# A decoder block on one core: the feed-forward by seven block products for eight

## The chip, the cores and the metric

The kernel runs on one core of a Trainium2 chip. The metric is the device time of one execution in microseconds (us). TensorE multiplies matrices out of on-chip memory into PSUM, VectorE and ScalarE do the elementwise work, GpSimd does a little of it, and SyncE issues most transfers between DRAM and on-chip memory. In the rows of a profile they are called PE, DVE, ACT, POOL and SP. PEld is the load of a matmul's stationary operand, which overlaps PE.

## The reference

One layer of a decoder over 512 tokens of width 2048: two token mixers side by side, an output projection, and a gated feed-forward of inner width 5632. The change touches the last part, from `w_out` on.

```python
def reference(x, norm_mix_g, w_in, sink_logits, w_branch_a, w_branch_b, w_out,
              norm_ffn_g, w_ffn_in, w_ffn_down, norm_final_g):
    ...
    x = x + (sigmoid(ga) * ya + sigmoid(gb) * yb) @ w_out
    h = rmsnorm(x, norm_ffn_g)
    gate, up = jnp.split(h @ w_ffn_in, 2, axis=-1)
    x = x + (silu(gate) * up) @ w_ffn_down
    return rmsnorm(x, norm_final_g)
```

All of it is float32. `x` is 512 x 2048, `w_ffn_in` 2048 x 11264, `w_ffn_down` 5632 x 2048.

## The kernel before

**Every product is three matmuls.** Each float32 operand is kept as a high part, rounded to the type fp32r, and the low part that is left over. A product is hi·hi + hi·lo + lo·hi. A weight block of 128 x 1024 elements (512 KB) is brought by one SP transfer (L130), cast to its high part by ACT (L134), and the low part is formed by DVE (L135). Three buffers each hold the raw block, its high and its low part (`wp`). `Weights.next` keeps two blocks ahead of the one in use. One such block feeds 24 matmuls of 512 columns in the feed-forward.

**Feed-forward.** The normalised `x2`, features on partitions, stands as sixteen pairs `fh`, `fl` of 128 x 512. The inner width is walked in five parts, `FF_PARTS` = 8, 8, 8, 10, 10 tiles of 128. In a part, `features` (L208 to L210) computes two tiles of gate and then two of up, with the weights stationary and the features moving. `scaled` (L353) multiplies by the reciprocal norm of each token, which `along_rows` had spread over all partitions as `inv2_bc`; ACT takes silu (L818), DVE multiplies (L824), ACT and DVE split the result into `ah` and `al` (L826, L827). Then `rows` (L722 to L724) multiplies `ah`, `al` (stationary) by the rows of `w_ffn_down` (moving), four token tiles for each of four column blocks, and DVE adds the four banks to `x2` (L843). The last column block of the last part is written out by hand: the weights are split ahead (`split_tail`), and token tile after token tile is finished, normalised and sent out (L858 to L864, `finish`).

**What sets the order.** The weights are planned as a list in the order of use. The program is recorded in code order and then put in an order by a scheduler, after which each engine runs its own rows strictly in that order; a row that waits holds up every row behind it on its engine. `later` and `gap` put small pieces of work between weight blocks.

**Before the feed-forward.** `w_out` is multiplied by `rows` for four column blocks n. After each block `x2` is added up (L753), squared (L730), transposed 128 x 128 by 128 x 128 (`turn_x1`; by DVE and copies for the first twelve feature tiles, by PE for the last four) and split into `fh`, `fl` (L254, L255).

On-chip memory: 79 slots of 128 x 512 in one pool (`tp`), constants in `cp`. PSUM has eight banks, four tagged "mm" and four "at".

Of the kernel before, what the change touches and what calls it, by code (L numbers as in the profile page):

```python
# [16 lines left out]
P = 128  # L17
T = 512
# [23 lines left out]
FF_PARTS = (8, 8, 8, 10, 10)  # L42
# [3 lines left out]
def kernel(  # L46
# [22 lines left out]
    tp = ctx.enter_context(tc.tile_pool(name="tp", bufs=79))  # L69
# [42 lines left out]
    class Weights:  # L112
# [11 lines left out]
        def split(self):  # L124
            w, k0, nk, c0, ncol = self.todo.popleft()
            raw = wp.tile([P, 1024], F32, tag="raw", name=uid("raw"))
            hi = wp.tile([P, 1024], F32R, tag="whi", name=uid("whi"))
            lo = wp.tile([P, 1024], F32R, tag="wlo", name=uid("wlo"))
            n = nk * ncol
            nc.sync.dma_start(  # L130
                out=raw[:, :n].rearrange("p (k c) -> p k c", k=nk),
                in_=w[k0 * P : (k0 + nk) * P, c0 : c0 + ncol].rearrange("(k p) c -> p k c", p=P),
            )
            nc.scalar.copy(hi[:, :n], raw[:, :n])  # L134
            nc.vector.tensor_tensor(out=lo[:, :n], in0=raw[:, :n], in1=f(hi[:, :n]), op=ALU.subtract)  # L135
            self.ready.append(
                (
                    hi[:, :n].rearrange("p (k c) -> p k c", k=nk),
                    lo[:, :n].rearrange("p (k c) -> p k c", k=nk),
                    nk,  # L140
                )
            )

        def next(self):
            while self.todo and len(self.ready) <= self.AHEAD:
                self.split()
            return self.ready.popleft()
# [28 lines left out]
    f0 = 0  # L176
    for p, nf in enumerate(FF_PARTS):
        for g in range(nf // 2):
            plan_cols(w_fi, KD, (f0 + 2 * g) * P)
            plan_cols(w_fi, KD, DFF + (f0 + 2 * g) * P)  # L180
        for n in range(4 if p < len(FF_PARTS) - 1 else 3):
            plan_rows(w_fd, f0, nf, n)
        f0 += nf
# [67 lines left out]
    def split_features(b, g):  # L251

        hi, lo = slot("fh", F32R), slot("fl", F32R)
        upper.append(nc.scalar.activation(out=hi, in_=b, func=AF.Copy, scale=g))  # L254
        nc.vector.scalar_tensor_tensor(out=lo, in0=b, scalar=g, in1=f(hi), op0=ALU.mult, op1=ALU.subtract)  # L255
        return hi, lo
# [70 lines left out]
    for b, base in enumerate((0, P)):  # L327
        df = const(f"dist{b}", 2 * P)
# [16 lines left out]
    inv_bc, invq_bc = const("inv_bc", T), const("invq_bc", T)  # L345
# [238 lines left out]
    corner = [[const(f"corner{e}{j}", 2 * P, F32R) for j in range(2)] for e in range(2)]  # L584
# [103 lines left out]
    for g in range(8):  # L688
# [11 lines left out]
        for m in range(2):  # L700
# [3 lines left out]
            mh[k], ml[k] = slot("mh", F32R), slot("ml", F32R)  # L704
# [27 lines left out]
    def turn_x1(k, tag):  # L732
        if k < KD - 4:
            z = slot("z")
            for t in range(NT):
                nc.vector.transpose(
                    z[:, t * P : (t + 1) * P], x2[t][k // 4][:, (k % 4) * P : (k % 4 + 1) * P]
                )
            fh[k], fl[k] = split_features(unblock(z, NT, 8), gcol[:, KD + k : KD + k + 1])
            return  # L740
        b = bank(tag)
        for t in range(NT):
            transpose(b[:, t * P : (t + 1) * P], x2[t][k // 4][:, (k % 4) * P : (k % 4 + 1) * P])
        fh[k], fl[k] = split_features(b, gcol[:, KD + k : KD + k + 1])

    for n in range(4):
        tag = ("mm", "at")[n % 2]
        for t in range(NT):
            x2[t][n] = load_after("x2", x[t * P : (t + 1) * P, n * T : (n + 1) * T], v)
        ob = [bank(tag) for _ in range(NT)]  # L750
        rows(KD, mh, ml, ob)
        for t in range(NT):
            nc.vector.tensor_tensor(out=x2[t][n], in0=x2[t][n], in1=ob[t], op=ALU.add)  # L753
            square_of(x2[t][n], ss2[:, 4 * t + n : 4 * t + n + 1])
        v = x2[0][n]
        for k in range(4 * n, 4 * n + 4):
            later(lambda k=k, tag=tag: turn_x1(k, tag), 4 if n < 3 else 2)

    def norm2():
        inv2 = const("inv2", NT)  # L760
        nc.vector.tensor_reduce(out=inv2, in_=ss2.rearrange("p (t c) -> p t c", t=NT), axis=AX.X, op=ALU.add)
        rsqrt_mean(inv2, inv2, NT, [small(s, NT) for s in ("rv", "rr", "rq")])
        nc.scalar.copy(inv2_bc, along_rows(inv2))

    inv2_bc = cp.tile([P, T], F32, tag="inv_bc", name="inv2_bc")


    later(norm2, 2)
    sst = const("sst", 4 * NT + 1)
    tail_w = []  # L770
    gf = [None] * 4

    def split_tail(k):

        raw = wp.tile([P, 1024], F32, tag="raw", name=uid("raw"))
        nc.sync.dma_start(
            out=raw.rearrange("p (k c) -> p k c", k=2),
            in_=w_fd[k * P : (k + 2) * P, 3 * T :].rearrange("(k p) c -> p k c", p=P),
        )
        for j in range(2):  # L780
            r = raw[:, j * T : (j + 1) * T]
            a, b = slot("dh", F32R), slot("dl", F32R)
            nc.scalar.copy(a, r)
            nc.vector.tensor_tensor(out=b, in0=r, in1=f(a), op=ALU.subtract)
            tail_w.append((a, b))

    def tail_next():
        if len(tail_w) < FF_PARTS[-1]:
            split_tail(KF - FF_PARTS[-1] + len(tail_w))

    def finish(t):

        tot, inv = small("tot", 1), small("inv3", 1)
        nc.vector.tensor_reduce(
            out=tot, in_=sst[:, 4 * t : 4 * t + (5 if t == NT - 1 else 4)], axis=AX.X, op=ALU.add
        )
# [8 lines left out]
    f0 = 0  # L805
    for p, nf in enumerate(FF_PARTS):
        last_part = p == len(FF_PARTS) - 1
        ah, al = [], []
        for g in range(nf // 2):
            gbk = [bank("mm") for _ in range(2)]  # L810
            features(KD, fh, fl, gbk)
            if p == 0 and g == 0:
                while pieces:
                    pieces.popleft()[1]()
            sl = []
            for m in range(2):
                v = scaled(gbk[m], inv2_bc)
                nc.scalar.activation(out=v, in_=v, func=AF.Silu)  # L818
                sl.append(v)
            ub = [bank("mm") for _ in range(2)]  # L820
            features(KD, fh, fl, ub)
            for m in range(2):
                u = scaled(ub[m], inv2_bc)
                nc.vector.tensor_tensor(out=u, in0=u, in1=sl[m], op=ALU.mult)  # L824
                a, b = slot("ah", F32R), slot("al", F32R)
                nc.scalar.copy(a, u)  # L826
                nc.vector.tensor_tensor(out=b, in0=u, in1=f(a), op=ALU.subtract)  # L827
                ah.append(a)
                al.append(b)
        if last_part:  # L830
            for n in range(4):
                gf[n] = load_after("gf", norm_final_g[n * T : (n + 1) * T].partition_broadcast(P), f(al[-1]))
        for n in range(4):
            tag = ("at", "mm")[n % 2]
            banks = [bank(tag) for _ in range(NT)]
            if last_part and n == 3:
                break
            if last_part and n >= 1:
                for k in range(nf // 2):
                    later(tail_next, 2)  # L840
            rows(nf, ah, al, banks)
            for t in range(NT):
                nc.vector.tensor_tensor(out=x2[t][n], in0=x2[t][n], in1=banks[t], op=ALU.add)  # L843
                if last_part:
                    square_of(x2[t][n], sst[:, 4 * t + n : 4 * t + n + 1])
                    nc.vector.tensor_tensor(out=x2[t][n], in0=x2[t][n], in1=gf[n], op=ALU.mult)
        if last_part:
            extra = bank("at")
            for t in range(NT):
                c = slice(t * P, (t + 1) * P)  # L850
                if t < NT - 1:
                    parts = [(banks[t], slice(0, T))]
                else:
                    parts = [(banks[t][:, : T // 2], slice(0, T // 2)), (extra[:, : T // 2], slice(T // 2, T))]
                for e, (b, cols) in enumerate(parts):
                    for k in range(nf):
                        wa, wb = tail_w[k]
                        mm(b, lhsT=ah[k][:, c], rhs=wa[:, cols], start=(k == 0), stop=False)  # L858
                        mm(b, lhsT=ah[k][:, c], rhs=wb[:, cols], start=False, stop=False)  # L859
                        mm(b, lhsT=al[k][:, c], rhs=wa[:, cols], start=False, stop=(k == nf - 1))  # L860
                    xt = x2[t][3][:, cols]
# [41 lines left out]
```

## Time and profile before

| | |
|---|---|
| time, median of 3 runs | 2655.57 us (2654.2 to 2655.95) |
| the profiled execution | 2655.02 us |
| its span in the trace | 2653.1 us, 1.9 us less than its time |
| feed-forward in the trace | from about 1185 us to about 2642 us |
| full-width matmuls of the feed-forward | 4224 in gate/up, 2112 in down |
| `w_ffn_in` loads | 176 of 512 KB |
| `w_ffn_down` loads | 88 of 512 KB |
| DMA traffic over the span | 284.18 MB, mean 107 GB/s |

The span is the time from the first to the last thing that the trace holds of this execution. Busy times are sums over an engine's instructions; several matmuls are in flight at once, so the mean duration of one (389 ns for 512 columns) is longer than the distance from one to the next. The distance is read from a stretch in which PE never pauses. "Idle before" is the time an engine stood still ahead of the rows of a group, and the name behind the arrow is what ended most of it.

### The profile page before, as it was taken

How to read it: one execution, taken by the hardware profiler on the slowest of the kernel's cores; microseconds unless marked ns; L12 is line 12 of the kernel's file. 1: busy time of each engine (PE TensorE's matmuls, PEld its weight loads, DVE VectorE, ACT ScalarE, POOL GpSimd, SP SyncE). 2: the span in 40 equal slices, each digit the busy share in tenths (PEclk: the TensorE clock that was granted, in tenths of full speed). 3: DMA queues.
4: the chain of work that ended last, by engine and by line, in shares of the span. 5: the costliest groups of instructions: out<-in, count | busy, mean ns of one | idle time of the engine just before them, and what ended most of it. 6: DMA issues, size and time to landing. Idle time of an engine off the chain costs nothing.

```text
span 2653.1 us, 32111 instructions
## 1 busy us (share of the span) xinstructions
PE 2623.9 (99%) x12183; PEld 2195.6 (83%) x12183; DVE 1379.9 (52%) x2730; ACT 1075.4 (41%) x2160; POOL 69.9 (3%) x141
## 2 busy tenths in 40 slices
PE   9999999999998999999999999999999999999998
PEld 8888878888887888888888888888888888888887
DVE  5688888888698443554333333333333333333343
ACT  6567767666576333553222222122212222122232
POOL 0000011111010000000000000000000000000000
PEclk9999999999999999999999999999999999999999
DMA  5333333323325444332332333333223332333342
GB/s 170 101 96 96 104 101 99 105 90 121 94 92 171 157 145 139 127 119 89 100 98 96 95 96 98 101 96 95 95 97 102 96 95 96 97 102 96 96 140 82
DMA packets 236475, 284.18 MB, mean 107 GB/s; under 512 B 9984, under 2 KB 187168, under 8 KB 236320
## 3 DMA queue, kind: packets, MB, share of 16 engines
q1 hardware_dynamic: 229200, 269.52, 32.1%
q10 hardware_dynamic: 7120, 12.61, 1.2%
q8 instruction: 95, 1.56, 0.2%
q14 instruction: 60, 0.49, 0.1%
HBM read 265.31 MB, written 16.78 MB: 106 GB/s over the span
## 4 chain that ended last, share of the span: by engine, by line
PE 68%; ACT 0%; DVE 0%; issue 0%; ACTq 0%
PE mm L210 14%; PE mm L209 14%; PE mm L208 14%; PE at L723 4%; PE at L724 4%; PE at L722 4%; PE mm L724 4%; PE mm L723 4%; PE mm L722 4%; PE mm L860 0%; PE mm L859 0%; PE mm L858 0%; PE at L97 0%; ACT turned L461 0%; PE at L860 0%; PE at L859 0%
## 5 line engine op out<-in xcount | busy, mean ns | idle before, releaser
L135 DVE TENSOR_TENSOR wlo<-raw,whi 128x1024 fp32r<-128x1024 f32 (+1 forms) x460 | 561.8, 1221 | 937.4 <-ACT whi L134 934.0
L134 ACT CAST whi<-raw 128x1024 fp32r<-128x1024 f32 (+1 forms) x460 | 483.7, 1052 | 1212.7 <-PE mm L209 698.9
L210 PE MATMUL mm<-fh,wlo 128*128 128x512 f32 x2304 | 898.2, 390 | 4.1 <-DVE wlo L135 3.9
L208 PE MATMUL mm<-fh,whi 128*128 128x512 f32 x2304 | 899.1, 390 | 0.0
L209 PE MATMUL mm<-fl,whi 128*128 128x512 f32 x2304 | 898.8, 390 | 0.0
L210 PEld LDWEIGHTS mm<-fh,wlo 128*128 128x128 f32 x2304 | 433.7, 188 | 96.5 <-DVE wlo L135 6.2
L209 PEld LDWEIGHTS mm<-fl,whi 128*128 128x128 f32 x2304 | 433.6, 188 | 88.1
L208 PEld LDWEIGHTS mm<-fh,whi 128*128 128x128 f32 x2304 | 433.6, 188 | 87.7
L461 ACT COPY turned<-z 32x128 f32<-32x128 f32 (+3 forms) x888 | 242.9, 274 | 113.9 <-DVE z L621 60.3
L461 DVE COPY turned<-z 32x128 f32<-32x128 f32 (+3 forms) x776 | 158.0, 204 | 10.8
L353 DVE TENSOR_TENSOR v<-mm,inv_bc 128x512 f32<-128x512 f32 x130 | 87.9, 688 | 119.4 <-PE mm L210 119.3
L722 PE MATMUL at<-whi,ah 128*128 128x512 f32 x352 | 136.9, 389 | 0.0
L723 PE MATMUL at<-wlo,ah 128*128 128x512 f32 x352 | 136.9, 389 | 0.0
L724 PE MATMUL at<-whi,al 128*128 128x512 f32 x352 | 136.9, 389 | 0.0
L722 PE MATMUL mm<-whi,ah 128*128 128x512 f32 x312 | 121.4, 389 | 0.0
L723 PE MATMUL mm<-wlo,ah 128*128 128x512 f32 x312 | 121.4, 389 | 0.0
L724 PE MATMUL mm<-whi,al 128*128 128x512 f32 x312 | 121.4, 389 | 0.0
L208 PE MATMUL mm<-yh,whi 128*128 128x512 f32 x256 | 99.6, 389 | 0.0
L209 PE MATMUL mm<-yl,whi 128*128 128x512 f32 x256 | 99.6, 389 | 0.0
L210 PE MATMUL mm<-yh,wlo 128*128 128x512 f32 x256 | 99.6, 389 | 0.0
L226 PE MATMUL mm<-whi,fl 128*128 128x256 f32 x320 | 90.5, 283 | 0.0
L225 PE MATMUL mm<-wlo,fh 128*128 128x256 f32 x320 | 90.5, 283 | 0.0
(193 smaller groups left out, 2710.3 us busy)
## 6 DMA issues: line engine op xcount, KB each, us to landing
raw<-in_w_ffn_in_dram SPq DMA_DIRECT2D x176, 512.0 KB, 3.6
raw<-in_w_in_dram SPq DMA_DIRECT2D x135, 512.0 KB, 3.7
raw<-in_w_ffn_down_dram SPq DMA_DIRECT2D x88, 512.0 KB, 3.6
raw<-in_w_out_dram SPq DMA_DIRECT2D x32, 512.0 KB, 3.6
x<-in_x_dram SPq DMA_DIRECT2D x32, 256.0 KB, 5.4
gate<-v ACTq DMA_DIRECT2D x32, 256.0 KB, 3.3
raw<-in_w_branch_a_dram SPq DMA_DIRECT2D x16, 512.0 KB, 3.4
raw<-in_w_branch_b_dram SPq DMA_DIRECT2D x16, 512.0 KB, 4.3
```

The lines of the kernel that those rows point to most:

```text
L134: nc.scalar.copy(hi[:, :n], raw[:, :n])
L135: nc.vector.tensor_tensor(out=lo[:, :n], in0=raw[:, :n], in1=f(hi[:, :n]), op=ALU.subtract)
L208: mm(b, lhsT=wh[:, kk, c], rhs=hi[k], start=(k == 0), stop=False)
L209: mm(b, lhsT=wh[:, kk, c], rhs=lo[k], start=False, stop=False)
L210: mm(b, lhsT=wl[:, kk, c], rhs=hi[k], start=False, stop=(k == nk - 1))
L225: mm(o, lhsT=hi[k][:, c], rhs=wl[:, kk, :], start=False, stop=False)
L226: mm(o, lhsT=lo[k][:, c], rhs=wh[:, kk, :], start=False, stop=last)
L353: nc.vector.tensor_tensor(out=v, in0=b, in1=by, op=ALU.mult)
L461: copy(t4[c * Q : (c + 1) * Q, :, r], z4[r * Q : (r + 1) * Q, :, c])
L722: mm(banks[t], lhsT=hi[k][:, c], rhs=wh[:, kk, :], start=(k == 0), stop=False)
L723: mm(banks[t], lhsT=hi[k][:, c], rhs=wl[:, kk, :], start=False, stop=False)
L724: mm(banks[t], lhsT=lo[k][:, c], rhs=wh[:, kk, :], start=False, stop=(k == nk - 1))
```

## The change

Both projections of the feed-forward are computed in 2 x 2 blocks by seven block products instead of eight (the form of Strassen's scheme that Winograd gave). Let the left operand be split into blocks by token half (256 tokens) and by even and odd k tile, and the right operand by even and odd k tile and by two column blocks of 512. `make_forms` builds the seven left-hand sums (`p1` to `p7`, each of them a 128 x 512 tile with high parts in one half and low parts in the other) from an even tile `e` and an odd tile `o`. On the weight side `plan_group` does the same on the raw blocks: it loads a block into `wx`, `wz` or `raw` (L217) and adds another in place (`plus`, L224), and each of the seven sums is then split as before (L150, L151). `product` multiplies one weight block by two forms into two token tiles: 12 matmuls. `ORDER` and `steps` interleave two of the products.

```diff
+    ORDER = (("p1", "p5"), ("p6", "p3"), ("p7", "p2"), ("p4",))
...
+                t = fp.tile([P, 1024], F32, tag=tag, name=uid(tag), bufs=4)
...
+        def item(name, j):
+            if name == "p1":
+                xt[j] = load("wx", j, 0, 0)
+            elif name == "p5":
+                plus(xt[j], load("raw", j, 0, 1))
+            elif name == "p6":
+                zt[j] = load("wz", j, 1, 1)
+                plus(xt[j], zt[j])
+            elif name == "p7":
+                plus(zt[j], load("raw", j, 0, 1))
+            elif name == "p2":
+                zt[j] = load("wz", j, 1, 0)
+            elif name == "p4":
+                plus(xt[j], zt[j])
+            return W.parts(zt[j] if name in ("p3", "p7", "p2") else xt[j])
...
+        u, c = [bank("mm") for _ in range(2)], None
+        for name, j in steps(nq):
+            if name in ("p5", "p2") and j == 0:
+                c = [bank("at") for _ in range(2)]
+            to = u if name in ("p1", "p6", "p7", "p4") else c
+            product([forms[2 * j + i][name] for i in range(2)], to, j == 0 and name in ("p1", "p5", "p2"), j == nq - 1)
+            if j == nq - 1:
+                after[name](to)
```

Gate and up now have tokens on partitions: the forms are stationary and the weights move. One of the two column blocks is gate, the other is up. There are eleven groups of 4 tiles of the inner width, 28 products each, and all of them stand before the first product of down. After a group DVE and ACT combine the partial sums (`copies`, `p3`, `p7`, `p2`, `p4`), scale by the token's norm (now a number per partition, so `inv2_bc` goes) and apply silu. PE transposes the result, 16 blocks a group (`turn`), and `make_forms` turns it into the forms for down. These 154 tiles of 256 KB are written to DRAM from POOL's queue and read back from it:

```diff
+            for res in st["gen"]:
+                name = list(res)[-1]
+                nc.gpsimd.dma_start(out=form_d[p][name], in_=res[name])
...
+        for name in FORMS:
+            for i in range(np):
+                if i % 2 == 0:
+                    res[i][name] = fp.tile([P, T], F32R, tag="fx", name=uid("fx"), bufs=21)
+                else:
+                    res[i][name] = slot("fx", F32R)
+                nc.gpsimd.dma_start(out=res[i][name], in_=form_d[p0 + i][name])
```

Down runs in four parts of 3, 3, 3 and 2 blocks of four k tiles, each for two pairs of column blocks: eight groups of 21 or 14 products. Each partial sum is added to `x2` or taken from it as it is done (`into`). The output tail by hand is gone (`split_tail`, `tail_next`); the last product of the last group serves two token tiles at once.

`x2` goes to DRAM after `w_out` (16 stores from POOL's queue) and comes back ahead of down. On-chip memory is laid out anew: `tp` has 47 slots, 32 slots of a second pool (`ep`) hold the operands of the early stages, and once these are done (`early.close()`) their room becomes the pool `fp`: four buffers each for `wx` and `wz`, and 21 form slots.

```diff
+    early.close()
+    fp = ctx.enter_context(tc.tile_pool(name="fp", bufs=1, side="right", reuse_waits="tile"))
...
+    W.fill()
+    late = [make_forms(xs2[2 * p], xs2[2 * p + 1], lambda name, p=p: form_slot(p, name)) for p in range(4, 8)]
+    for _ in range(2):
+        for p, gen in enumerate(late):
+            xforms[4 + p] = next(gen)
+    for gen in late:
+        later(lambda gen=gen: [None for _ in gen], 1)
```

In count: 792 matmuls of 512 columns go, 176 transposes of 128 x 128 come. The three places below show how the rows move.

**DVE inside gate/up.** Before, this engine splits weight blocks one after the other and between them finishes two tiles (v is a tile of gate or up, al its low part):

```order
L135 TENSOR_TENSOR wlo_12727<-raw_12725,whi_12726 128x1024
L353 TENSOR_TENSOR v_12755<-mm_12633,inv_bc 128x512
L824 TENSOR_TENSOR v_12755<-v_12755,v_12627 128x512
L135 TENSOR_TENSOR wlo_12773<-raw_12771,whi_12772 128x1024
L827 TENSOR_TENSOR al_12759<-v_12755,ah_12758 128x512
L353 TENSOR_TENSOR v_12762<-mm_12634,inv_bc 128x512
```

Now, in the second group of gate/up, where `p7` and `p2` are multiplied and the sums for `p4` are made (L224 adds the blocks, L940 takes the finished product from the partial sum t):

```order
L151 TENSOR_TENSOR wlo_13500<-wz_13300,whi_13499 128x1024
L151 TENSOR_TENSOR wlo_13519<-wz_13326,whi_13518 128x1024
L940 TENSOR_TENSOR t_13476<-at_13203,t_13476 128x512
L940 TENSOR_TENSOR t_13477<-at_13204,t_13477 128x512
L224 TENSOR_TENSOR wx_13090<-wx_13090,wz_13555 128x1024
L151 TENSOR_TENSOR wlo_13540<-wz_13356,whi_13539 128x1024
L224 TENSOR_TENSOR wx_13108<-wx_13108,wz_13594 128x1024
L151 TENSOR_TENSOR wlo_13558<-wz_13555,whi_13557 128x1024
L224 TENSOR_TENSOR wx_13134<-wx_13134,wz_13612 128x1024
L151 TENSOR_TENSOR wlo_13577<-wz_13412,whi_13576 128x1024
L224 TENSOR_TENSOR wx_13178<-wx_13178,wz_13632 128x1024
L151 TENSOR_TENSOR wlo_13597<-wz_13594,whi_13596 128x1024
```

Of the names `wz`, 13300, 13326, 13356 and 13412 are the four blocks of `p7` (j = 0 to 3), and 13555, 13594, 13612 and 13632 are the blocks of `p2` that are loaded into the same four buffers. The sums for `p4` (L224 into `wx`) stand ahead of splits for `p7` and `p2`; the last of them reads block 13632, whose buffer is the one that the row before the last L224 still reads.

**ACT from `w_out` to gate/up.** Before, the squares of the last column block (L730), the last four feature tiles (L254) and the casts of the coming weight blocks (L134) alternate:

```order
L134 CAST whi_12183<-raw_12182 128x1024
L730 ACTIVATE j_12173,ss_10793<-x_1813_11812 128x512
L730 ACTIVATE j_12176,ss_10793<-x_1814_11815 128x512
L234 ACT_TABLE_LOAD
L234 ACTIVATE rr_12275<-rv_12274 128x4
L254 ACTIVATE fh_12205<-at_12200,gcol 128x512
L254 ACTIVATE fh_12220<-at_12215,gcol 128x512
L134 CAST whi_12240<-raw_12239 128x1024
```

Now the squares are L854, the scaled tiles L875, the forms L278 and the casts of weights L150. The first cast of a feed-forward block stands here:

```order
L854 ACTIVATE j_12269,ss_10815<-x_1833_11930 128x512
L854 ACTIVATE j_12273,ss_10815<-x_1834_11933 128x512
L875 ACTIVATE turned_12281<-at_12276,gcol 128x512
L875 ACTIVATE turned_12288<-at_12283,gcol 128x512
L875 ACTIVATE turned_12295<-at_12290,gcol 128x512
L875 ACTIVATE turned_12302<-at_12297,gcol 128x512
L356 ACT_TABLE_LOAD
L356 ACTIVATE rr_12312<-rv_12311 128x4
L278 CAST fx_12344<-turned_12281 128x256
L150 CAST whi_12322<-wx_12320 128x1024
L278 CAST fx_12347<-turned_12295 128x256
L150 CAST whi_12328<-wx_12326 128x1024
```

Before, three blocks of `w_ffn_in` (12106, 12136 and 12182) are cast ahead of the last square. Now none is: they wait for buffers that stand in the memory of the operands of `w_out`.

**DVE at the same place, now.** Between the splits of the first three weight blocks (wlo) stand the sums d and the low parts fx of the forms of `x2`, which every group of gate/up uses:

```order
L151 TENSOR_TENSOR wlo_12329<-wx_12326,whi_12328 128x1024
L279 TENSOR_TENSOR fx_12352<-d_12350,fx_12352 128x256
L279 TENSOR_TENSOR fx_12357<-d_12355,fx_12357 128x256
L279 TENSOR_TENSOR fx_12362<-d_12360,fx_12362 128x256
L279 TENSOR_TENSOR fx_12539<-d_12350,fx_12539 128x256
L224 TENSOR_TENSOR wx_12320<-wx_12320,raw_12557 128x1024
L359 SCALAR_TENSOR_TENSOR rr_12312<-rr_12312,rq_12313 128x4
L279 TENSOR_TENSOR fx_12367<-d_12365,fx_12367 128x256
L289 TENSOR_TENSOR d_12657<-d_12365,turned_12302 128x256
L151 TENSOR_TENSOR wlo_12335<-wx_12332,whi_12334 128x1024
L279 TENSOR_TENSOR fx_12544<-d_12542,fx_12544 128x256
L279 TENSOR_TENSOR fx_12654<-d_12365,fx_12654 128x256
```

Before, the rows between two splits at this place were the low parts of the last four feature tiles (L255), which is all that was left to form:

```order
L255 SCALAR_TENSOR_TENSOR fl_12206<-at_12200,gcol,fh_12205 128x512
L255 SCALAR_TENSOR_TENSOR fl_12221<-at_12215,gcol,fh_12220 128x512
L135 TENSOR_TENSOR wlo_12241<-raw_12239,whi_12240 128x1024
L255 SCALAR_TENSOR_TENSOR fl_12236<-at_12230,gcol,fh_12235 128x512
L255 SCALAR_TENSOR_TENSOR fl_12257<-at_12251,gcol,fh_12256 128x512
```

The forms of `x2` stand among the splits now, over forty rows of them (L279, L284, L286, L289, L291) before the first `p6` block is split.

More of the change, by code (lines that the diff above doesn't have):

```diff
@@ L40 @@
 O_GB = 6656
-FF_PARTS = (8, 8, 8, 10, 10)
 @with_exitstack
@@ new lines, in product @@
+    def product(forms, banks, first, last):
+        wh, wl, _ = W.next()
+        for kk in range(2):
+            a = forms[kk]
+            for t in range(2):
+                hi, lo = a[:, t * P : (t + 1) * P], a[:, (2 + t) * P : (3 + t) * P]
+                one, end = first and kk == 0, last and kk == 1
+                mm(banks[t], lhsT=hi, rhs=wh[:, kk, :], start=one, stop=False, skip_group_check=True)
+                mm(banks[t], lhsT=hi, rhs=wl[:, kk, :], start=False, stop=False, skip_group_check=True)
+                mm(banks[t], lhsT=lo, rhs=wh[:, kk, :], start=False, stop=end, skip_group_check=True)
+        gap()
@@ L752 @@
         for t in range(NT):
[L753 to L770, printed above, removed]
-    gf = [None] * 4
[L773 to L785, printed above, removed]
@@ L787, in tail_next @@
-    def tail_next():
-        if len(tail_w) < FF_PARTS[-1]:
-            split_tail(KF - FF_PARTS[-1] + len(tail_w))
+            nc.vector.tensor_tensor(out=xr[t], in0=xr[t], in1=ob[t], op=ALU.add)
+            square_of(xr[t], ss2[:, 4 * t + n : 4 * t + n + 1])
+            nc.gpsimd.dma_start(out=x2_d[t][n], in_=xr[t])
+        v = xr[0]
+        if n < 3:
+            for k in range(4 * n, 4 * n + 4):
+                later(lambda k=k, xr=xr, tag=tag: turn_x1(k, xr, tag), 4)
+    while pieces:
+        pieces.popleft()[1]()
@@ L803, in finish @@
             nc.sync.dma_start(out=out[t * P : (t + 1) * P, m * T : (m + 1) * T], in_=x2[t][m])
[L805 to L830, printed above, removed]
-            for n in range(4):
[L832 to L861, printed above, removed]
-                    nc.vector.tensor_tensor(out=xt, in0=xt, in1=b, op=ALU.add)
-                    square_of(xt, sst[:, 4 * t + 3 + e : 4 * t + 4 + e])
-                    nc.vector.tensor_tensor(out=xt, in0=xt, in1=gf[3][:, cols], op=ALU.mult)
-                finish(t)
-        f0 += nf
@@ new lines, in down, with into, fn @@
+    def down(nq, forms, n, last):
+        def into(half, col, op, done=False, end=False):
+            def fn(b):
+                for i in range(2):
+                    t, m = 2 * half + i, n + col
+                    o = x2[t][m]
+                    nc.vector.tensor_tensor(out=o, in0=o, in1=b[i], op=op)
+                    if last and done:
+                        square_of(o, sst[:, 4 * t + m : 4 * t + m + 1])
+                        nc.vector.tensor_tensor(out=o, in0=o, in1=gf[m], op=ALU.mult)
+                    if last and end:
+                        finish(t)
+            return fn
+        add, sub = ALU.add, ALU.subtract
+        group(
+            nq,
+            forms,
+            {
+                "p1": into(0, 0, add),
+                "p5": into(1, 1, add),
+                "p6": into(0, 1, sub),
+                "p3": into(0, 1, add, True),
+                "p7": into(1, 1, sub, True),
+                "p2": into(0, 0, add, True, n == 2),
+                "p4": into(1, 0, add, True, n == 2),
+            },
+        )
@@ L869 @@
+    p0 = 0
+    for part, nq in enumerate(DOWN_PARTS):
+        last = part == len(DOWN_PARTS) - 1
+        dforms = load_forms(p0, 2 * nq)
+        if last:
+            for n in range(4):
+                gf[n] = slot("gf")
+                nc.sync.dma_start(out=gf[n], in_=norm_final_g[n * T : (n + 1) * T].partition_broadcast(P))
+        for n in (0, 2):
+            down(nq, dforms, n, last)
+        while pieces:
+            pieces.popleft()[1]()
+        p0 += 2 * nq
 _INS = [
```

217 lines of the change are left out of this document (176 added, 41 removed).

## The prediction

> **What bounds the kernel now.** First the page's busy shares and its chain of work that ended last, to see which engine sets the end; then one undisturbed stretch of the feed-forward.
>
> ```profile
> span 2653.1 us, 32111 instructions
> PE 2623.9 (99%) x12183; PEld 2195.6 (83%) x12183; DVE 1379.9 (52%) x2730; ACT 1075.4 (41%) x2160; POOL 69.9 (3%) x141
> PE 68%; ACT 0%; DVE 0%; issue 0%; ACTq 0%
> ```
>
> PE is busy for 99% of the span and the chain names hardly anything else. The windows view (length, busy time and instructions of each engine, granted clock, DMA share, GB/s) gives the price of a matmul and the load of the other engines:
>
> ```profile
> 0.00:14.00 14.00, 8.21 (x36) 6.72 (x36) 5.78 (x10) 6.32 (x8) 2.91 (x12) 1.00 0.82 268
> 14.00:30.00 16.00, 16.00 (x94) 13.49 (x93) 10.01 (x13) 13.92 (x38) 0.00 (x0) 1.00 0.88 292
> 810.00:820.00 10.00, 6.20 (x29) 4.93 (x28) 8.91 (x32) 7.11 (x23) 1.29 (x2) 1.00 0.38 128
> 820.00:830.00 10.00, 8.89 (x32) 6.80 (x31) 8.17 (x27) 6.60 (x21) 0.00 (x0) 0.83 0.32 103
> 1200.00:1220.00 20.00, 20.00 (x100) 16.59 (x99) 12.24 (x22) 10.44 (x18) 0.00 (x0) 1.00 0.25 80
> 1290.00:2500.00 1210.00, 1210.00 (x5340) 1002.26 (x5339) 422.45 (x445) 278.31 (x301) 0.00 (x0) 1.00 0.31 97
> ```
>
> From 1290 to 2500 us PE never pauses: 1210.00 us for 5340 matmuls is 0.2266 us each, at full clock, with DVE busy 35% and ACT 23%. So before, a matmul less is 0.2266 us less. The question is whether DVE, ACT and the loads still keep up when each block must be added up as well.
>
> **What goes.** 792 matmuls x 0.2266 = **-179.5 us**, all from a stretch in which PE is the limit. The hand-written tail's half-width matmuls and the four of `along_rows` are about -1.
>
> **What comes on PE.** 176 transposes. The chain of waits shows four between two matmuls:
>
> ```profile
> 1211.35 0.44 PE at L97 x4
> ```
>
> 0.11 us each, **+19.4 us**. If PE were all, the span would be 2653.1 - 179.5 - 1 + 19.4 = 2492.0 us.
>
> **What comes on DVE.** Rows by line, with shapes apart (count, busy, mean ns, idle before), and four rows of the timeline (start, length):
>
> ```profile
> L135 DVE TENSOR_TENSOR wlo<-raw,whi 128x1024 fp32r<-128x1024 f32 x458 | 560.5, 1224 | 936.7 <-ACT whi L134 933.3
> L353 DVE TENSOR_TENSOR v<-mm,inv_bc 128x512 f32<-128x512 f32 x130 | 87.9, 688 | 119.4 <-PE mm L210 119.3
> L488 DVE SCALAR_TENSOR_TENSOR s<-dist,at 128x256 f32<-128x256 f32 x64 | 23.0, 416 | 1.0 <-PE at L484 0.9
> 1262.02 1.05 ACT L134 CAST whi<-raw 128x1024 fp32r<-128x1024 f32 x1 [4.39 <-PE mm L209]
> 1263.11 1.23 DVE L135 TENSOR_TENSOR wlo<-raw,whi 128x1024 fp32r<-128x1024 f32 x1 [4.21 <-ACT whi L134]
> 1295.71 1.23 DVE L135 TENSOR_TENSOR wlo<-raw,whi 128x1024 fp32r<-128x1024 f32 x1
> 1296.85 0.69 DVE L827 TENSOR_TENSOR al<-v,ah 128x512 fp32r<-128x512 f32 x1
> ```
>
> A group of gate/up has 28 products of 12 matmuls, 2.72 us each, 76.1 us, and with its transposes 78. DVE does 28 splits and 16 block additions (44 x 1.22), 10 rows of 512 (x 0.69) and 22 rows of 256 (x 0.42): 70 us. Neighbours that don't wait for each other start closer than their length (1295.71 to 1296.85 is 1.14 for a 1.23); by that pitch it is 64. So DVE goes from 35% to 82 to 90%: below PE on average, but with no room for waits, and it does its rows in order. ACT has 28 casts of 1.05, ten copies and four silus near 0.6 and 14 small casts near 0.41, 44 us a group, and sets nothing. I take PE as the bound between the places below.
>
> **The stall that comes back in each group.** The rows of DVE that the change shows say where. The last addition for `p4` needs block j = 3 of `p2`, whose buffer is free only when `p7`'s j = 3 is split; behind that addition wait the splits for `p2`. The loads:
>
> ```profile
> raw<-in_w_ffn_in_dram SPq DMA_DIRECT2D x176, 512.0 KB, 3.6
> raw<-in_w_branch_b_dram SPq DMA_DIRECT2D x2, 512.0 KB, 5.4
> sg<-gate SPq DMA_DIRECT2D x32, 256.0 KB, 4.3
> gate<-v ACTq DMA_DIRECT2D x32, 256.0 KB, 3.3
> ...
> DMA packets 4454, 6.68 MB, mean 334 GB/s; under 512 B 367, under 2 KB 2023, under 8 KB 4453
> ```
>
> (512 KB takes 3.6 us at the 97 GB/s of before; the second row and the last are the answer for 840 to 860 us, where it takes 5.4 at 334 GB/s.) From the start of `p7` j = 0, in us: split of `p7` j = 2 done at 3.9, its buffer's next block lands at 7.5, added by 8.7, split of `p7` j = 3 done at 9.95, next block lands at 13.55, added by 14.8, split of `p2` j = 1 done at 16.05. PE wants that at 5 x 2.72 + 0.45 = 14.05: it waits **2.0 us**. Two load times lie in series, so with 5.4 us loads it is 5.6. A group moves 20 x 512 KB and 14 x 256 KB in 78 us, some 185 GB/s, between the two rows; loads of about 4.1 us give 3.0. Eleven groups: **+33 us (0 to 62)**; zero, if DVE is further ahead than this walk has it. Where `p1`, `p5` and the 22 form rows of the group before meet, DVE is short by 0 to 1 us a group: **+4 (0 to 11)**.
>
> **From `w_out` to gate/up.** Before, PE doesn't notice this place (1200 to 1220 us is full). Now ACT must first do four squares, four scaled tiles, the table load and three small casts, and DVE the forms:
>
> ```profile
> L730 ACT ACTIVATE j<-x 128x512 f32<-128x512 f32 x4 | 2.5, 628 | 3.1 <-DVE x L753 3.1
> L254 ACT ACTIVATE fh<-at,gcol 128x512 fp32r<-128x512 f32 x4 | 2.6, 686 | 1.7 <-PE at L97 1.7
> L234 ACT ACT_TABLE_LOAD x1 | 1.3, 1283 | 0.0
> L730 ACT ACTIVATION_READ_ACCUMULATOR j<-x 128x1 f32 x4 | 0.7, 186 | 0.0
> ```
>
> On ACT 2.5 + 0.7 + 2.6 + 1.3 + about 1.5 of small rows and the cast make 9.6 us of PE standing still. Then DVE sets the pace: up to the split of the first `p6` block stand four additions to `x2`, 17 block rows and 44 rows of 256 and a few tiny ones, 2.8 + 20.7 + 18.5 + 0.9 = 43 us by lengths and 38 by pitches, where eight products last 21.8. So PE is 15 to 21 us late there, the ACT wait within it; **+19 (10 to 25)**.
>
> The clock belongs to this place. From 810 to 820 us PE stood for 3.8 us, and the next 10 us were granted 0.83: 1.7 us. I add **+1.7** once. The Trainium skill has a rule for it ("TensorE: Matmul & The Clock Gate", "What's actually happening"): an idle window of about 3.4 us halves the clock, until a window as long was busy. The two rows agree with it, but the standstill at the start of the program (0 to 14 us) shows no such drop; without the rule this term is 0.
>
> **The early stages** keep their rows; the 79 slots are 47 and 32 now. I cost them at nothing, +-2 us for transfers that SP issues in another order in the first 50 us.
>
> **From gate/up to down.** On POOL's queue the reads for even tiles stand ahead of those for odd ones, and the last even read waits for a slot that the last product of gate/up frees. The first odd read is then needed half a product (1.4 us) into down. No DMA of this size from POOL is in the trace; the nearest rows are the 3.3 and 4.3 us above, so 2 to 3 us late, and with DVE's forms of the last group **+4 (0 to 8)**. The Trainium skill ("DMA: Bandwidth & Descriptors", "Anatomy of one DMA — SWDGE (gpsimd) path") puts such a transfer at 2.0 us and the bytes over 436 GB/s, an estimate of 2.6 us here and 1 us less in the sum; no row of before can show it.
>
> **Down.** Groups of 21 products last 57.1 us and DVE has 33 x 1.22 + 14 x 0.69 = 50 in them, with a buffer of `wz` to spare. The two last groups, of 14 products (38.1 us), have 22 x 1.22 + 22 x 0.69 = 42 with the final gains: 1 to 4 us late each. While the next part's forms are read, loads compete (14 to 30 us shows 292 GB/s at 0.88). **+7 (0 to 20)**. Stores of forms and of `x2` hide behind PE, which reads them one part or more later; without that cover each would cost its 3.3 us.
>
> **The tail.** Before:
>
> ```profile
> 2644.35 0.42 DVE L862 TENSOR_TENSOR x<-x,at 128x256 f32<-128x256 f32 x1 [1.85 <-PE at L860]
> 2647.08 1.33 ACT L800 ACTIVATE x<-x,inv 128x512 f32<-128x512 f32 x2 [0.81 <-DVE inv L238]
> ```
>
> From the last addition to the end 8.75 us. Now two token tiles of 512 columns end at once: one more addition, square and product with the gain, **+1.5**.
>
> **Sum.** 2492.0 + 33 + 4 + 19 + 1.7 + 4 + 7 + 1.5 = 2562 us of span, and 1.9 us that lay around it before: **2564 us**. The profiled run (2655.02) lies 0.55 under the median of the runs, which is within this work's grain.
>
> **Rivals.**
>
> *The cover holds.* DVE runs far enough ahead for the loads to be hidden, and only the start of gate/up (10) and the tail cost: 2492 + 10 + 1.5 + 1.9 = 2505. For it: in 1290 to 2500 us DVE is idle for two thirds of the time. Against: that reserve is what the additions use up.
>
> *Slow loads and the clock.* Loads take the 5.4 us seen at 334 GB/s, so each group stands for 5.6 us, which is longer than the 3.8 after which the clock fell, and loses 1.7 more: 11 x (5.6 + 1.7 - 3.0) = 47, **2611**. The clock rule named above says just this of a wait that returns in each group.
>
> *DVE and ACT in lockstep; slower than before.* If additions don't run ahead, each product with one takes 1.22 + 1.09 (1262.02 to 1263.11) + 1.23 = 3.54 us instead of 2.72. There are 16 x 11 + 88 = 264 of them: +216, and 2492 + 216 + 19 + 4 + 7 + 1.5 + 1.9 = 2741. It decides from about three fifths of the additions on, where the time passes 2656. Against: the rows in the change put the next addition ahead of the current split, so DVE has work while ACT casts.
>
> **Chances.** The forecast's case, 2535 to 2590: 45%. Cover, below 2535: 22%. Slow loads, 2590 to 2635: 17%. Lockstep in full or part, above 2635: 16%, of which 3 still faster, 2 about equal and 11 slower. The range runs from the cover's 2505 to 2635, which leaves the last case out and a little below. About 0.2% (5 us) is what a measurement of this kernel can tell from none: faster 87%, same 2%, slower 11%.
>
> **What would show it.** PE busy near 2490 us less the tail, with idle time of some 60 to 70 us that ends mostly on `wlo`; DVE at 75% or more of the span; about 3 us of PE waiting once in each group, at the second block of `p2`; 20 us at the start of gate/up; loads of `wx`, `wz` and `raw` near 4 us. It is wrong if `p2` doesn't wait, if loads take over 5 us, or if PE waits inside every product for `wlo`.

## The result and the profile after

The changed kernel takes **2561.35 us** (2560.66 to 2562.37, 4 runs) against 2655.43: a ratio of 0.9647, 95% interval 0.963 to 0.9663. The forecast was 2564. The sum came out right, but two of its largest parts did not: a stall that it priced at 33 us isn't there, and 39 us of slower matmuls are, which it didn't have. That the two are nearly the same size is luck.

The changed kernel's page: the span, the engines' busy times (share of the span, instructions), the chain of work that ended last.

```profile
span 2559.2 us, 33175 instructions
PE 2512.7 (98%) x11529; PEld 2063.9 (81%) x11529; DVE 1981.0 (77%) x3457; ACT 1377.3 (54%) x2626; POOL 241.7 (9%) x465
PE 62%; issue 2%; DVE 1%; ACT 1%; DMA 1%; POOL 0%; ACTq 0%; POOLq 0%; DVEq 0%
```

PE is busy for 2512.7 us. Before it was 2623.9, and with 792 matmuls less and the transposes it should be near 2463. So 50 us went neither into waits nor into work that the prediction had counted: PE was busy for longer with the same instructions. Of these, 39 are matmuls that start further apart at full clock, and some 11 are stretches at a lower clock; both follow below.

The windows of the changed kernel (length; busy time and instructions of PE, PEld, DVE, ACT, POOL; granted clock, DMA share, GB/s): the start of gate/up, the rest of gate/up, the start of down, the rest of down.

```profile
1217.00:1270.00 53.00, 42.65 (x170) 32.95 (x169) 45.21 (x77) 31.62 (x60) 1.72 (x4) 0.90 0.45 149
1270.00:2090.00 820.00, 820.00 (x3652) 670.11 (x3651) 683.25 (x781) 426.01 (x574) 83.06 (x157) 1.00 0.62 185
2090.00:2150.00 60.00, 51.45 (x211) 40.59 (x210) 44.10 (x59) 25.40 (x39) 23.97 (x45) 0.91 1.02 324
2150.00:2530.00 380.00, 380.00 (x1640) 307.24 (x1639) 318.38 (x323) 148.18 (x153) 57.04 (x107) 1.00 0.68 211
```

From 1270 to 2090 us, ten and a half groups, PE never stands still, though DVE is busy for 83% of that time. From 1200 us on, all the waiting is at the two transitions. In the last row no transposes remain, and 1640 matmuls take 380 us: 0.2317 each, at full clock, where before it was 0.2266.

What PE waited for from 1200 us on (us in total, times, longest):

```profile
PE mm L253 <- ACT whi L150: 9.5, 2, 5.4
PE at L254 <- DVE wlo L151: 4.7, 2, 3.3
PE mm L253 <- DMA fx<-f1p: 3.8, 1, 3.8
```

And the loads, issue to landing, all of them slower than the 3.6 us of before:

```profile
raw<-in_w_ffn_in_dram SPq DMA_DIRECT2D x88, 512.0 KB, 3.7
wz<-in_w_ffn_in_dram SPq DMA_DIRECT2D x88, 512.0 KB, 4.4
...
wz<-in_w_ffn_down_dram SPq DMA_DIRECT2D x44, 512.0 KB, 5.4
```

### The profile page after: what moved, and what is told of

Its sections match the earlier page's. It is cut to its first block, busy times and chain, and to the rows that moved or that the text cites. A ratio compares the mean times of both kernels' runs of the same rounds, so it can differ in the third digit from the quotient of the medians.

```text
span 2559.2 us, 33175 instructions
## 1 busy us (share of the span) xinstructions
PE 2512.7 (98%) x11529; PEld 2063.9 (81%) x11529; DVE 1981.0 (77%) x3457; ACT 1377.3 (54%) x2626; POOL 241.7 (9%) x465
## 3 DMA queue, kind: packets, MB, share of 16 engines
q1 hardware_dynamic: 204400, 308.32, 38.7%
## 4 chain that ended last, share of the span: by engine, by line
PE 62%; issue 2%; DVE 1%; ACT 1%; DMA 1%; POOL 0%; ACTq 0%; POOLq 0%; DVEq 0%
PE mm L253 9%; PE mm L255 9%; PE mm L254 9%; PE at L253 7%; PE at L255 7%; PE at L254 7%; PE mm L331 3%; PE mm L330 3%; PE mm L332 3%; PE mm L848 1%; PE mm L847 1%; PE mm L846 1%; PE at L848 1%; PE at L847 1%; PE at L846 1%
## 5 line engine op out<-in xcount | busy, mean ns | idle before, releaser
L150 ACT CAST whi<-wx 128x1024 fp32r<-128x1024 f32 x264 | 277.3, 1051 | 331.4 <-PE mm L255 150.6
L254 PE MATMUL mm<-wlo,fx 128*128 128x512 f32 x1056 | 418.1, 396 | 0.2 <-DVE wlo L151 0.2
L255 PE MATMUL mm<-whi,fx 128*128 128x512 f32 x1056 | 417.0, 395 | 0.0
L151 DVE TENSOR_TENSOR wlo<-wx,whi 128x1024 fp32r<-128x1024 f32 x264 | 322.7, 1223 | 115.4 <-ACT whi L150 114.1
L151 DVE TENSOR_TENSOR wlo<-raw,whi 128x1024 fp32r<-128x1024 f32 (+1 forms) x201 | 244.1, 1215 | 191.6 <-ACT whi L150 189.6
L253 PE MATMUL mm<-whi,fx 128*128 128x512 f32 x1056 | 377.1, 397 | 13.3 <-ACT whi L150 9.5
L150 ACT CAST whi<-wz 128x1024 fp32r<-128x1024 f32 x198 | 208.0, 1050 | 288.4 <-PE mm L255 142.8
L332 PE MATMUL mm<-fh,wlo 128*128 128x512 f32 x896 | 356.0, 397 | 1.4 <-DVE wlo L151 1.4
L330 PE MATMUL mm<-fh,whi 128*128 128x512 f32 x896 | 355.7, 397 | 0.0
L331 PE MATMUL mm<-fl,whi 128*128 128x512 f32 x896 | 355.5, 397 | 0.0
L150 ACT CAST whi<-raw 128x1024 fp32r<-128x1024 f32 (+1 forms) x201 | 209.7, 1044 | 225.6 <-PE mm L331 142.1
L254 PE MATMUL at<-wlo,fx 128*128 128x512 f32 x792 | 311.6, 393 | 4.7 <-DVE wlo L151 4.7
L255 PE MATMUL at<-whi,fx 128*128 128x512 f32 x792 | 312.4, 394 | 0.0
L151 DVE TENSOR_TENSOR wlo<-wz,whi 128x1024 fp32r<-128x1024 f32 x198 | 240.6, 1222 | 53.6 <-ACT whi L150 53.4
L253 PE MATMUL at<-whi,fx 128*128 128x512 f32 x792 | 281.2, 395 | 0.5 <-ACT whi L150 0.5
L253 PEld LDWEIGHTS mm<-whi,fx 128*128 128x128 f32 x1056 | 198.6, 189 | 57.8 <-ACT whi L150 10.4
L254 PEld LDWEIGHTS mm<-wlo,fx 128*128 128x128 f32 x1056 | 199.9, 189 | 45.6 <-DVE wlo L151 1.3
L255 PEld LDWEIGHTS mm<-whi,fx 128*128 128x128 f32 x1056 | 199.7, 189 | 45.2
```

The source lines that it names most:

```text
L253: mm(banks[t], lhsT=hi, rhs=wh[:, kk, :], start=one, stop=False, skip_group_check=True)
L254: mm(banks[t], lhsT=hi, rhs=wl[:, kk, :], start=False, stop=False, skip_group_check=True)
L255: mm(banks[t], lhsT=lo, rhs=wh[:, kk, :], start=False, stop=end, skip_group_check=True)
L330: mm(b, lhsT=wh[:, kk, c], rhs=hi[k], start=(k == 0), stop=False)
L331: mm(b, lhsT=wh[:, kk, c], rhs=lo[k], start=False, stop=False)
L332: mm(b, lhsT=wl[:, kk, c], rhs=hi[k], start=False, stop=(k == nk - 1))
```

## The experiments

### Why a matmul takes longer

The slower matmuls start before the feed-forward, in stages that the change leaves as they were. One of these is `w_out`, the same 80 us of it before and after:

```profile
1090.00:1170.00 80.00, 80.00 (x355) 66.26 (x354) 44.85 (x116) 40.32 (x89) 0.00 (x0) 1.00 0.37 125
```

```profile
1090.00:1170.00 80.00, 80.00 (x345) 64.25 (x344) 52.79 (x143) 47.81 (x114) 2.16 (x4) 1.00 0.39 129
```

Both are full, at full clock, but ten matmuls fewer fit in. The rows by line show the same thing as duration, 389 ns for this product before (L722, the first fence) and 395 now (L846), and also where it does not occur: the products of the branch weights (`yh`) keep their 389.

```profile
L722 PE MATMUL mm<-whi,mh 128*128 128x512 f32 x128 | 49.8, 389 | 0.0
```

```profile
L330 PE MATMUL mm<-yh,whi 128*128 128x512 f32 x256 | 99.6, 389 | 0.0
...
L846 PE MATMUL mm<-whi,mh 128*128 128x512 f32 x128 | 50.6, 395 | 0.0
```

What tells these apart is where an operand lies. By the addresses that the built programs give their tiles, every tile that a 512-column matmul read before started 32 bytes past a multiple of 256 in its partition. With the change, the left part of memory (weights, `tp`) starts at multiples of 256, and the right part (`ep` with `mh` and the early features, then `wx`, `wz` and 21 form slots) at 224 past one. 5862 of the 9984 matmuls of 512 columns then read one operand from each. In the trace they start 0.2333 us apart in the mean, and those with both operands in one part 0.227 in the median, as before. At 0.0066 us each that is 38.7 us in all.

**The right-hand part moved by 32 bytes**, then **by 224**:

```diff
+    edge = ctx.enter_context(tc.tile_pool(name="edge", bufs=1, side="right"))
+    nc.vector.memset(edge.tile([P, 8], F32, tag="edge", name="edge"), 0.0)
     early = ctx.enter_context(ExitStack())
```

> The changed kernel with everything in the right-hand part of on-chip memory (operands of the early stages, later wx, wz and 21 form slots) moved by 32 bytes, so that every matmul operand starts at a multiple of 64 bytes. Theory A (start offset): a 512-column matmul takes 0.2267 us when both operands have the same start offset modulo 64 bytes and 0.2333 when one is 32 off; 5862 of the changed kernel's 9984 are mixed, 38.7 us, which go: 2561 - 39 = 2522 (2515 to 2530), and the w_out matmuls (L846 to L848) show 389 ns instead of 395. Theory B (place or traffic: that part of memory, or DMA and DVE at work, slows PE): nothing changes, 2561 within 3.

Measured: 2545.98 us, ratio to before 0.9588 (0.9574 to 0.9602). Neither theory: 15 us went, not 39 and not none. The window of `w_out` shows a middle value:

```profile
1090.00:1170.00 80.00, 80.00 (x351) 65.67 (x350) 53.65 (x143) 47.99 (x115) 2.49 (x5) 1.00 0.41 133
```

The operands now agreed modulo 64 but were 64 apart modulo 256; the early features, as the moving operand, still started 0.233 apart, the forms and `mh`, as the stationary one, 0.229. So a larger modulus, with `[P, 56]` for `[P, 8]`:

> As the kernel with the right-hand part moved by 32 bytes, but by 224, so that all matmul operands have the same start offset modulo 256 bytes (moved by 32 they were equal modulo 64 only, and 64 apart modulo 128). Theory A, mended (the offsets must agree modulo more than 64, at most 256): every matmul of 512 columns takes 0.2267 us, 2561 - 39 = 2522 (2516 to 2530). Theory A with 512 as the modulus: the mixed ones stay at 0.229 to 0.233, 2535 to 2561. Theory B (place): 2546 as with 32, or no change at all.

Measured: **2531.86 us**, ratio 0.9537 (0.9523 to 0.9551), 29.5 less than the changed kernel. All slow matmuls are gone:

```profile
1090.00:1170.00 80.00, 80.00 (x355) 66.24 (x354) 55.71 (x163) 49.55 (x118) 4.32 (x8) 1.00 0.46 150
```

That is 9 us short of 39, and just outside the expected range. Some 5 of the 9 are waits that came back: PE stands still for 51.5 us of the span (2529.2 less 2477.7 of busy time), and for 46.5 in the changed kernel. Most of that is in the first 880 us, where PE stands still for 20.4 us before, 15.1 in the changed kernel and 18.6 here (500 + 290 + 90 less the busy times of these windows): where PE waits for other engines anyway, slower matmuls had cost nothing. The other 4 us stay open.

**The reverse, in the kernel before**: its 79 slots moved against the weight buffers by 32, 128 and 256 bytes, and nothing else.

```diff
+    edge = ctx.enter_context(tc.tile_pool(name="edge", bufs=1))
+    nc.vector.memset(edge.tile([P, 8], F32, tag="edge", name="edge"), 0.0)
     tp = ctx.enter_context(tc.tile_pool(name="tp", bufs=79))
```

> The kernel before, with its 79 slots moved by 32 bytes against the weight buffers, and nothing else. Theory A (start offset): 10536 of its 10746 matmuls of 512 columns become mixed, 0.0066 us each, +70: 2655 + 70 = 2725 (2710 to 2735). Theory B (place or traffic): 2655 within 3.

> The kernel before with its slots moved by 128 bytes against the weight buffers (by 32 it took 2714). If the offsets must agree modulo 128 or less: 2655 within 3. If modulo 256 or more: 10536 matmuls take 0.2290 to 0.2333, 2680 to 2725.

> The kernel before with its slots moved by 256 bytes against the weight buffers (by 32 and by 128 it took 2714 and 2712). Start offsets that agree modulo 256 are enough: 2655 within 3. If moving the slots costs by itself, or the modulus is larger: 2680 to 2715.

Measured: 2714.25 us by 32 (ratio 1.0223, 1.0206 to 1.024), 2712.19 by 128 (1.0217, 1.0202 to 1.0232), and 2654.69 by 256 (1.0001, 0.9991 to 1.001). The window of `w_out` for 32, then for 256:

```profile
1090.00:1170.00 80.00, 80.00 (x345) 64.41 (x344) 45.69 (x125) 42.08 (x96) 0.00 (x0) 1.00 0.36 119
```

```profile
1090.00:1170.00 80.00, 80.00 (x355) 66.24 (x354) 45.23 (x116) 40.62 (x91) 0.00 (x0) 1.00 0.36 122
```

A kernel without any right-hand part, with the DMA and DVE work that it always had, becomes 59 us slower when a spare tile of 32 bytes is put between two pools, and not at all when it is 256 bytes. That leaves nothing of the rival (place or traffic). The 59 falls short of 70 in part for the same reason as above: moved by 32 bytes, PE is busy for 63.6 us more (2687.5 against 2623.9) and stands still for 4.8 us less.

### Why the stall of each group isn't there

The prediction let the last block of `p2` wait for the split of `p7`'s last block, since it took the one's buffer for the other's. The part on the change says so too, and it is wrong there: block 13632 was given the buffer of block 13555 (`p2`, j = 0), not that of 13412. DVE in one group of the changed kernel (start, length, idle before):

```profile
1682.33 1.23 DVE L224 TENSOR_TENSOR wx<-wx,wz 128x1024 f32<-128x1024 f32 x1 [1.19 <-DMA wz<-in_w_ffn_in_dram]
1683.47 1.22 DVE L151 TENSOR_TENSOR wlo<-wz,whi 128x1024 fp32r<-128x1024 f32 x1
1684.89 1.23 DVE L224 TENSOR_TENSOR wx<-wx,wz 128x1024 f32<-128x1024 f32 x1 [0.20 <-DMA wz<-in_w_ffn_in_dram]
```

The middle row is the split of `p7`, j = 3; it ends at 1684.69. The block that is added at 1684.89 can't have been loaded in the 0.20 us between: its load had left after the split of `p2`, j = 0, three rows earlier. The first row's wait of 1.19 us is the one that the walk had right.

**As it was walked**: the same order on DVE, but with each block of `p2` loaded into the tile that `p7` of the same j has left.

```diff
...
+            elif name == "p2" and j == 1:
+                for i in (1, 2, 3):
+                    reload(i)
+                with tc.issue_after(plus(xt[3], zt[3]).ins):
+                    return W.parts(zt[1])
...
```

> The changed kernel, but in gate/up the block j = 3 of p2 is loaded into the buffer of p7's j = 3 (in the changed kernel it takes that of p2's j = 0), and the last addition for p4 is put ahead of the split of p2's j = 1, as the prediction walked it. If the prediction's walk was right but for the buffer: PE waits 2.0 us (loads of 3.6) to 3.6 us (loads of 4.4) in each of 11 groups, +22 to +40: 2583 to 2601, with idle time that ends on wlo. If DVE has a reserve that the walk missed: 2561 within 4.

Measured: 2596.96 us, ratio 0.978 (0.9766 to 0.9795), 35.6 more than the changed kernel. The same three rows of the same group, and PE's waits over the whole run:

```profile
1696.29 1.23 DVE L224 TENSOR_TENSOR wx<-wx,wz 128x1024 f32<-128x1024 f32 x1 [1.35 <-DMA wz<-in_w_ffn_in_dram]
1697.44 1.22 DVE L151 TENSOR_TENSOR wlo<-wz,whi 128x1024 fp32r<-128x1024 f32 x1
1702.39 1.22 DVE L224 TENSOR_TENSOR wx<-wx,wz 128x1024 f32<-128x1024 f32 x1 [3.73 <-DMA wz<-in_w_ffn_in_dram]
```

```profile
PE at L268 <- DVE wlo L151: 30.9, 13, 3.5
```

4.7 us of it were there in the changed kernel; the other 26.2 are 2.4 us for each of 11 groups, inside the 2.0 to 3.6 of the walk, though the loads took 4.4 us here too, for which the walk has 3.6. The way of counting was right, if too long by about a third, and the dependency that it counted along was not in the kernel. Of the other 9.4 us, 2.6 are further waits (PE stands still for 75.3 us of the span, 28.8 more than in the changed kernel), and some 7 are clock: the granted clock fell to half for 3.41 us behind four of the eleven waits, an estimate of 1.7 us each.

### The start of gate/up

**The last forms spread**: of `x2`'s pairs 4 to 7, five forms each, one at a time between the products of the first group and not all behind the first product.

```diff
-    for gen in late:
-        later(lambda gen=gen: [None for _ in gen], 1)
+    for _ in range(5):
+        for gen in late:
+            later(lambda gen=gen: next(gen), 1)
```

> The changed kernel, with the last five forms of x2's pairs 4 to 7 made one at a time between the products of the first group, instead of all behind the first product. If DVE's form rows make the second part of the standstill from w_out to gate/up: the waits on wlo of 1.6 and 3.5 us near 1237 and 1244 us shrink, and with them the matmuls at half clock behind the longer one: 2561 - 9 = 2552 (2549 to 2556). If ACT's chain alone sets it: 2561 within 3, with the first wait of 5.4 us as it was in both cases.

Measured: 2556.41 us, ratio 0.9627 (0.9612 to 0.9641), 4.9 less than the changed kernel (the intervals of the two ratios overlap by a little) and about half of the 9 that were expected. The trace has the reason: the wait of 5.4 us on ACT stays, and those on `wlo` (4.7 us) shrink to 0.6, while 1.4 us of smaller waits come up in other rows.

```profile
PE mm L253 <- ACT whi L150: 9.5, 2, 5.4
...
PE at L254 <- DVE wlo L151: 0.6, 2, 0.3
```

So both of the causes that the prediction named act, one after the other: first ACT's chain, then DVE's form rows.

### The start of down

POOL's queue in the changed kernel (start, length, idle before), the last even reads and the first odd one, and four pieces of the chain of work that ended last:

```profile
2098.90 0.54 POOL L999 DMA_DIRECT2D fx<-f0p  x1 [7.70 <-PE mm L255]
2100.30 0.54 POOL L999 DMA_DIRECT2D fx<-f2p  x1 [0.86 <-PE mm L255]
2102.12 0.54 POOL L999 DMA_DIRECT2D fx<-f4p  x1 [1.28 <-PE mm L255]
2102.64 0.54 POOL L999 DMA_DIRECT2D fx<-f1p  x1
```

```profile
2102.64 6.53 DMA fx<-f1p
...
2127.93 8.34 DMA f20p<-fo
...
2137.71 0.41 ACT fo L278
2138.12 0.96 ACT whi L150
```

As forecast, the first odd read stands behind the last even one, which waits for the last products of gate/up. It then takes 6.5 us, where the rows that the prediction went by had 3.3 and 4.3. Twenty more reads follow it, and behind them, from 2127.93, the stores of the last group's forms; ACT needs a slot that one of these holds (2137.71), and a cast of weights stands behind ACT's row (2138.12). That second standstill (4.1 us) the prediction did not have.

**Odd reads on SP's queue**:

```diff
...
-                nc.gpsimd.dma_start(out=res[i][name], in_=form_d[p0 + i][name])
+                (nc.sync if i % 2 else nc.gpsimd).dma_start(out=f(res[i][name]), in_=form_d[p0 + i][name])
```

> The changed kernel, with the form reads of odd tiles issued from SP's queue and not from POOL's (the forms in DRAM are typed float32 for it; the bytes are the same). If POOL's queue makes the standstill from gate/up to down (3.8 us for the first odd read, then 4.2 us for a cast behind form stores that stand behind the reads), it shrinks to 2 us or less, with the matmuls at half clock behind it: 2561 - 10 = 2551 (2547 to 2556). If the slots of the odd reads come free only then, or SP's weight loads are held up instead: 2561 or slower.

Measured: 2562.17 us, ratio 0.9651 (0.9635 to 0.9667): no gain. The second standstill is gone, but the first is 12.8 us long, since SP brings back `x2` first:

```profile
2101.43 11.36 SPq L987 DMA_DIRECT2D x<-x  x16
2113.11 0.32 SPq L999 DMA_DIRECT2D fx<-f1p  x1
```

**The reads in the last group of gate/up**, on POOL's queue as they were, recorded behind that group's `p3`:

```diff
...
         def p3(b):
             for i in range(2):
                 nc.vector.tensor_tensor(out=st["t"][i], in0=b[i], in1=st["t"][i], op=ALU.subtract)
+            if g == NPAIR // 2 - 1:
+                first.append(load_forms(0, 2 * DOWN_PARTS[0]))
...
```

> The changed kernel with the form reads of down's first part put into the last group of gate/up (behind its p3), still on POOL's queue; so none of the odd reads stands behind the last even one, and the last form stores stand right behind the reads. If the place of the reads in the queues makes the standstill from gate/up to down: its two waits (3.8 and 4.2 us) go, and the matmuls at half clock behind them: 2561 - 11 = 2550 (2547 to 2555). If what ends last there is DVE or the slots: 2561 within 3.

Measured: 2548.82 us, ratio 0.9601 (0.9587 to 0.9615), 12.5 less than the changed kernel. The 60 us around that place, of which PE stood still for 8.5 before, and with a clock of 0.91:

```profile
2078.00:2138.00 60.00, 59.36 (x266) 48.04 (x265) 52.51 (x64) 29.98 (x40) 12.90 (x25) 1.00 0.94 320
```

### Together

The right-hand part moved by 480 bytes, the forms spread, odd reads on SP:

> The changed kernel with three things together: the right-hand part moved by 480 bytes (start offsets equal modulo 512), the last forms of x2 spread over the first group, odd form reads on SP's queue. By theory A: -39 for the offsets, -5 as the spread forms measured, and what the odd reads give (0 to -10): 2561 - 39 - 5 - 8 = 2509 (2500 to 2520). By theory B 2546 or more.

Measured: 2527.62 us, ratio 0.9522 (0.9508 to 0.9536). It misses its range, and the reads are most of why: the 12.5 us wait for the first odd read is in this run too. With the reads in the last group of gate/up in its place:

> The changed kernel with the right-hand part moved by 480 bytes, the last forms of x2 spread over the first group, and the form reads of down's first part in the last group of gate/up. 2532 with the move alone (by 224), 5 less for the spread forms, 11 less for the reads: 2516 (2510 to 2522).

Measured: **2515.58 us** (2514.61 to 2515.91), ratio 0.9476 (0.9462 to 0.949), the fastest version, 46 us under the changed kernel.

```profile
span 2513.8 us, 33198 instructions
PE 2471.2 (98%) x11529; PEld 2061.3 (82%) x11529; DVE 1976.7 (79%) x3458; ACT 1378.3 (55%) x2626; POOL 242.4 (10%) x465
```

PE's busy time is 2471 us, 8 above the 2463 of the count.

## Why the prediction was right, step by step

| step | predicted, us | shown by the runs, us |
|---|---|---|
| 792 matmuls fewer, at the old 0.2266 | -179.5 | -179.5, once offsets agree |
| 176 transposes | +19.4 | about 19, four adding some 0.43 |
| stall of each group at `p2` | +33 | 0 |
| `p1`, `p5` and forms | +4 | 0 |
| start of gate/up | +19 and +1.7 of clock | 10.4 of standing, 5.3 of clock |
| start of down | +4 | 8.6 of standing, 5.4 of clock |
| rest of down | +7 | 0 |
| tail | +1.5 | +3.8 |
| early stages | 0, +-2 | -5.3 of standing |
| matmuls with unlike offsets | not there | +39 |

The standing and the clock at the two starts are read from the windows: 53 less 42.65 and 0.10 of 53 at the first, 60 less 51.45 and 0.09 of 60 at the second. The 39 is the 38.7 from above. The measured column gives a span of 2560 from 2653.1; the trace has 2559.2. The 792 are counted in full widths: 762 matmuls of 512 columns go, and the old tail's 60 of 256.

**The step that failed is the recurring stall.** The prediction took 33 of the 70 us that it put on top of PE's work from it, and its size was about right for a dependency that isn't there. The run that builds this dependency in costs 35.6 us. What let the sum come out was luck: the row at the end of the table is of nearly the same size. Of the rivals, "the cover holds" described the steady part of gate/up better than the forecast did, but its 2505 was out of reach with these offsets.

**Averages held where walks didn't.** DVE at 82 to 90% in gate/up was forecast, 83% was measured, and PE was the bound. The slower rival, lockstep, is excluded by 820 us without a pause.

**The starts** were right in mechanism, and too large and too small in size. At gate/up the prediction took DVE as 15 to 21 us late; PE stood for 10.4, and the clock took 5.3, three times the 1.7. At down it had one queue's order right and missed what stands behind the reads.

**The early stages** were costed at nothing because their rows are the same. Their rows are; the addresses in them are not, and no view of the order shows that.

The Trainium skill's clock rule ("TensorE: Matmul & The Clock Gate", "What's actually happening": an idle window of about 3.4 us halves the clock) is borne out in the length of the window, but the window needn't be idle throughout. In these traces the granted clock changes only at steps of 3.41 us. Here are three waits of the run with the stall built in (1.9, 3.3 and 3.5 us), cut at these steps, two rows for each:

```profile
1373.09:1376.50 3.41, 1.49 (x7) 0.93 (x6) 2.59 (x3) 1.05 (x1) 0.00 (x0) 1.00 0.04 12
1376.50:1379.91 3.41, 3.41 (x9) 2.63 (x10) 3.24 (x4) 0.00 (x0) 0.00 (x0) 0.50 0.70 200
1536.92:1540.34 3.42, 1.70 (x8) 1.06 (x6) 0.81 (x1) 0.73 (x1) 0.00 (x0) 1.00 0.26 96
1540.34:1543.75 3.41, 1.80 (x8) 1.50 (x9) 3.41 (x5) 0.32 (x1) 0.00 (x0) 1.00 0.21 34
1868.00:1871.42 3.42, 0.92 (x4) 0.79 (x5) 3.34 (x3) 1.04 (x1) 0.00 (x0) 1.00 0.01 2
1871.42:1874.83 3.41, 3.41 (x10) 2.66 (x9) 2.49 (x4) 0.43 (x1) 0.00 (x0) 0.50 0.91 280
```

What counts is how long PE stands still within one step. The wait of 1.9 us lies in one step, and the next runs at half clock; the wait of 3.3 us is split into 1.7 and 1.6, and no clock is lost. In the thirteen traces, 50 steps at full clock have more than 1.87 us of standing, and every one is followed by a step at half clock; of those with less than 1.68 us none is. So whether a wait of 2 to 3.3 us costs clock depends on where it falls.

The prediction also took the start of the program for a standstill without a drop, since the windows view prints 1.00 there. The trace holds no clock before about 11 us, and the rows do show the drop: the same transposes start 0.21 us apart at 7 us and 0.11 apart at 16 (start, length of the group, idle before; kernel before).

```profile
7.19 1.97 PE L97 MATMUL at<-ident,x 128*128 128x128 f32 x8 [1.31 <-DMA x<-in_x_dram]
15.67 0.82 PE L97 MATMUL at<-ident,x 128*128 128x128 f32 x6
```

## What to carry to other kernels

When pools are laid out anew, compare the start addresses of what each matmul reads, modulo 256 bytes, before trusting that an untouched stage keeps its time; a spare tile sets it right. When the sum of a forecast agrees with the clock on the wall, check its terms one by one all the same: a full stretch of PE in which fewer matmuls fit shows in no list of waits. Follow a wait along the buffer that was really given, not along the one that the loop suggests.

## What the runs showed of the hardware

- A matmul of 512 columns (fp32r, 128 x 128 stationary) starts every 0.227 us when both operands have the same start offset modulo 256 bytes. With 32 or 128 bytes between them, whichever of the two is ahead, it is 0.233; with 64, 0.229 (the stationary one at 192, the moving one at 0) or 0.233 (the other way round). The cause inside the chip is open; that it is the offsets and not the place is shown by the kernel before, moved by 32 and by 256.
- Reads of 256 KB issued in a row on POOL's queue leave every 0.53 us at first (2102.12, 2102.64). The odd ones of down's first part, issued back to back beside the 16 loads of `x2`, took 10.5 to 10.7 us in the median; the even ones, which are issued further apart, took 4.2 to 5.2. Stores of 256 KB from the same queue took 2.3 to 3.1 in the first nine groups of gate/up.
- A step of 3.41 us at full clock in which PE stands still for more than 1.87 us is followed by one at half clock, and one with less than 1.68 us is not (thirteen traces).
